# A hybrid trunk layer on one core: the order of its instructions found with another model of the machine

## The chip, the cores and the metric

The kernel runs on one core of a Trainium2 chip. The metric is the device time of one execution in microseconds; the time before is the median of three runs. A profile is one further execution, recorded by the hardware profiler. The engines are TensorE (PE in the profile, its weight loads PEld), VectorE (DVE), ScalarE (ACT), GpSimd (POOL) and SyncE (SP), whose queue issues nearly all the transfers of this kernel.

## The reference

One layer of a streaming encoder over 1024 positions and 1024 channels, in float32:

```python
h = rms_norm(x, norm1_w)
q, k, v, g_ret, x_lru, y_lru, gate_ret, gate_lru = split(h @ w_in)
o = head_group_norm(chunkwise_retention(rotary(q), rotary(k), v), ret_gn_w)
y_a = (o * silu(g_ret)) @ w_ret_o
hl = rg_lru(causal_depthwise_conv(x_lru, ...), ...)
y_b = (hl * gelu(y_lru)) @ w_lru_o
mix = sigmoid(gate_ret + b0) * y_a + sigmoid(gate_lru + b1) * y_b
x = x + mix @ w_out
gate, val = split(rms_norm(x, norm2_w) @ ffn_w_up)
x = x + (gelu(causal_depthwise_conv(gate, ...)) * val) @ ffn_w_down
return rms_norm(x, norm_f_w)
```

Retention has four heads and is done in chunks with a state carried over; the recurrence (`rg_lru`) has block-diagonal gates and a scan over positions. The inner width of the last block is 3072.

## The kernel before

**Precision and products.** Every large product splits both operands in a high part (rounded to the fp32r format) and a low part (the rest): `split` (L164 to L169) does one cast on ScalarE (L167) and one subtraction on VectorE (L168). Three matmuls (high times high, high times low, low times high) then stand for one in float32. Tiles are 128 x 512.

**Jobs.** The work is a list of jobs, each a 256 x 1024 piece of output from a 256-column piece of a weight matrix: 28 jobs of the input projection, four for each of the two branch outputs, 24 up jobs (one 128-wide piece of the gate and one of the value) and 12 down jobs. A standard job (`mm_std`, L316) takes 96 matmuls at L330. Most are fast ones (`mm_fast`, L377): a Strassen-like scheme of seven products instead of eight on 2 x 2 blocks, 84 matmuls at L387, 12 for each product. It needs sums of blocks (L246 to L262 on VectorE for weights; `tsets`, L539 to L556, or `x_sums` for the other operand) and combines products: `keep` (L399 to L403) copies a PSUM bank on ScalarE (L402), `more` adds what is accumulated (L408), `total` (L411 to L414) adds a bank on VectorE (L413). After a copy the same bank goes on accumulating the next-but-one product. There are six banks for jobs and two for the rest (tile `a`). There are 61 fast jobs in all.

**Weights.** `loads` (L199) fetches raw blocks over SyncE's queue (L208), `preps` (L224) splits them; `pump` keeps up to six raw and seven split blocks ahead in 22 buffers `w`. All other tiles live in 81 buffers `u`; the buffer that each takes is chosen by the kernel's Python code while it writes the program.

**Background work.** After a job its `post` may leave a generator in `back`: the recurrence (`lru_block`, matmuls at L814, the product stored at L853), rotary, retention and their output. `advance` writes some of it between the products of later jobs. Operands for the next stage come from `builders`: `operand` loads tiles (L997 from the stored branch output, L1230 from the down weights) and splits them, and writes the sums. `build` and `need` do this, and `keep`, `total` and the weights' `pump` after the first job do their part, inside `hp()`, which raises the priority by an offset of 1500 instructions.

**After the branches.** The merge projection (L1182) adds the input and stores the sum, then comes the second norm with its transposes (L513). In the up stage `post_ff` (L1207 to L1224) does the convolution (L1212, L1215, L1217), GELU (L1218) and the product (L1219) and stores it through GpSimd's queue (L1220). The down stage loads those as "weights" (L208) and accumulates three groups of four jobs over the stored sum; the last group ends with the final norm (L1286 to L1302).

**What sets the order.** The program is written as one list of instructions. When the `TileContext` closes, the toolchain gives each engine and queue its own list: it runs the program through a model of the machine and puts down each instruction when, by that model, the data that it reads is there and the buffer that it writes is free; among several, the one with the higher priority goes first (program order, moved by `hp()`). Waits are then added where one engine depends on another. Within a queue the order is fixed from then on.

## Time and profile before

| | |
|---|---|
| median of three runs | 1673.02 us (1672.82, 1673.02, 1676.43) |
| the profiled execution | 1675.42 us |
| its span, first to last instruction | 1673.6 us |
| mean granted TensorE clock | 0.994 |
| instructions | 21183 |
| moved by transfers | 225.97 MB, 135 GB/s |

The span is what the trace covers; the 1.82 us between it and the execution's own time lie around it. Busy time of an engine is the time in which at least one of its instructions is recorded; for TensorE records overlap, since matmuls are pipelined. In lists of instructions, `x` is the count of merged ones, and the square bracket gives the time that the engine stood idle before the first of them, with what ended it. A line such as `ACT u L402 <- PE g L387` means: ScalarE's instruction of line 402 waited for TensorE's of line 387. `SPq` is an instruction that issues a transfer.

### The profile page before, as it was taken

How to read it: one execution, taken by the hardware profiler on the slowest of the kernel's cores; microseconds unless marked ns; L12 is line 12 of the kernel's file. 1: busy time of each engine (PE TensorE's matmuls, PEld its weight loads, DVE VectorE, ACT ScalarE, POOL GpSimd, SP SyncE). 2: the span in 40 equal slices, each digit the busy share in tenths (PEclk: the TensorE clock that was granted, in tenths of full speed). 3: DMA queues.
4: the chain of work that ended last, by engine and by line, in shares of the span. 5: the costliest groups of instructions: out<-in, count | busy, mean ns of one | idle time of the engine just before them, and what ended most of it. 6: DMA issues, size and time to landing. Idle time of an engine off the chain costs nothing.

```text
span 1673.6 us, 21183 instructions
## 1 busy us (share of the span) xinstructions
PE 1627.2 (97%) x7224; PEld 1332.6 (80%) x7224; DVE 1289.9 (77%) x2366; ACT 886.4 (53%) x1480; POOL 40.7 (2%) x60
## 2 busy tenths in 40 slices
PE   8999999999999999999999999999999999999997
PEld 6888788888888877887778788888888887777776
DVE  8998768666888889857862796777767777878886
ACT  7654444535678877753530564444444455444554
POOL 0001000000000000000000000000000000000000
PEclk9999999999999999999999999999999999999999
DMA  7243212131333348656463022222222237687851
GB/s 293 89 154 97 86 54 89 51 95 45 113 114 105 122 140 267 210 166 232 154 209 107 32 95 82 82 82 82 89 82 82 92 122 229 224 260 243 260 193 76
DMA packets 120524, 225.97 MB, mean 135 GB/s; under 512 B 14048, under 2 KB 14176, under 8 KB 120416
## 3 DMA queue, kind: packets, MB, share of 16 engines
q1 hardware_dynamic: 116192, 210.99, 39.1%
q0 software_dynamic: 4224, 13.64, 2.1%
q8 instruction: 56, 0.92, 0.2%
q14 instruction: 52, 0.43, 0.1%
HBM read 164.80 MB, written 54.53 MB: 131 GB/s over the span
## 4 chain that ended last, share of the span: by engine, by line
PE 50%; DVE 8%; DMA 6%; ACT 3%; issue 2%; SPq 0%; DVEq 0%; ACTq 0%
PE g L387 36%; PE g L330 7%; PE g L1182 4%; DMA u<-w_dn 2%; DVE u L168 2%; PE a L814 2%; DVE w L168 1%; DMA w<-ff_d 1%; DMA x_d<-u 1%; DVE u L797 1%; ACT u L167 1%; DVE u L413 1%; DMA u<-u_d 1%; PE a L513 0%; DMA u<-w_out 0%
## 5 line engine op out<-in xcount | busy, mean ns | idle before, releaser
L387 PE MATMUL g<-u,w 128*128 128x512 f32 x5124 | 1204.7, 393 | 20.1 <-ACT u L402 9.7
L387 PEld LDWEIGHTS g<-u,w 128*128 128x128 f32 x5124 | 958.9, 188 | 224.6 <-ACT u L402 14.8
L167 ACT CAST w<-w 128x512 fp32r<-128x512 f32 x471 | 291.3, 621 | 359.7 <-PE g L387 280.6
L168 DVE TENSOR_TENSOR w<-w,w 128x512 fp32r<-128x512 f32 x471 | 322.6, 686 | 90.0 <-ACT w L167 85.4
L330 PE MATMUL g<-u,w 128*128 128x512 f32 x960 | 227.2, 394 | 2.8 <-ACT u L167 2.8
L167 ACT CAST u<-u 128x512 fp32r<-128x512 f32 x232 | 139.3, 620 | 150.1 <-DVE u L552 16.1
L330 PEld LDWEIGHTS g<-u,w 128*128 128x128 f32 x960 | 181.3, 190 | 41.9 <-ACT u L167 3.2
L168 DVE TENSOR_TENSOR u<-u,u 128x512 fp32r<-128x512 f32 x232 | 154.5, 687 | 38.8 <-ACT u L167 25.9
L413 DVE TENSOR_TENSOR u<-g,u 128x512 f32<-128x512 f32 x183 | 125.6, 686 | 57.0 <-PE g L387 43.5
L402 ACT COPY u<-g 128x512 f32<-128x512 f32 x183 | 106.4, 582 | 73.8 <-PE g L387 73.7
L1182 PE MATMUL g<-u,u 128*128 128x512 f32 x384 | 90.1, 392 | 2.5 <-ACT u L167 1.6
L1182 PEld LDWEIGHTS g<-u,u 128*128 128x128 f32 x384 | 71.3, 188 | 18.4 <-ACT u L167 2.0
L1215 DVE SCALAR_TENSOR_TENSOR u<-u,par,u 128x511 f32<-128x511 f32 (+1 forms) x96 | 71.6, 747 | 6.2 <-ACT u L1212 5.5
L1220 POOL DMA_DIRECT2D ff_d<-u x48 | 36.2, 753 | 1271.0 <-DVE u L1219 1271.0
L246 DVE TENSOR_TENSOR w<-w,w 128x512 f32<-128x512 f32 x61 | 42.1, 690 | 20.6 <-DMA w<-w_up 12.6
L814 PE MATMUL a<-u,u 128*128 128x512 f32 x192 | 48.8, 394 | 4.3 <-ACT u L167 3.5
L1184 DVE TENSOR_TENSOR u<-g,u 128x512 f32<-128x512 f32 x16 | 11.1, 691 | 49.3 <-PE g L1182 49.3
L1212 ACT ACTIVATE u<-u,par 128x512 f32<-128x512 f32 x48 | 39.1, 817 | 15.7 <-DVE u L413 15.7
L814 PEld LDWEIGHTS a<-u,u 128*128 128x128 f32 x192 | 35.5, 188 | 14.3 <-ACT u L167 5.6
L249 DVE TENSOR_TENSOR w<-w,w 128x512 f32<-128x512 f32 x61 | 42.0, 688 | 0.9
L262 DVE TENSOR_TENSOR w<-w,w 128x512 f32<-128x512 f32 x61 | 41.9, 686 | 0.4
L255 DVE TENSOR_TENSOR w<-w,w 128x512 f32<-128x512 f32 x61 | 41.8, 685 | 0.3
(173 smaller groups left out, 1151.2 us busy)
## 6 DMA issues: line engine op xcount, KB each, us to landing
w<-w_in SPq DMA_DIRECT2D x112, 256.0 KB, 2.7
w<-w_up SPq DMA_DIRECT2D x96, 256.0 KB, 2.6
u<-w_dn SPq DMA_DIRECT2D x96, 256.0 KB, 4.0
u<-x_d SPq DMA_DIRECT2D x56, 256.0 KB, 5.3
x_d<-u SPq DMA_DIRECT2D x48, 256.0 KB, 3.3
ff_d<-u POOLq DMA_DIRECT2D x48, 256.0 KB, 2.5
w<-ff_d SPq DMA_DIRECT2D x48, 256.0 KB, 3.8
u<-x SPq DMA_DIRECT2D x32, 256.0 KB, 5.3
```

Source lines behind the costliest of these rows:

```text
L167: S.copy(hi, src)
L168: V.tensor_sub(lo, src, hi.bitcast(F32))
L246: V.tensor_add(s1, a21, a22)
L249: V.tensor_sub(s1, s1, a11)
L262: V.tensor_sub(s1, a12, s1)
L330: PE.matmul(ps[h], w[a][:, c], o[b], start=n == 0, stop=n == 23)
L387: PE.matmul(bank, w[a][:, c], need(op, (bn, j))[b], start=first and n == 0, stop=n == 11, skip_group_check=True)
L402: S.copy(u, bank)
L413: V.tensor_add(u, bank, u)
L814: PE.matmul(ps, wg[g][a][:, cs], xs[k][b], start=q == 0, stop=q == 5)
L1182: PE.matmul(ps, o[a][:, 128 * t:128 * t + 128], wo[k][b], start=n == 0, stop=n == 23)
L1215: V.scalar_tensor_tensor(c[:, s:], src[:, :TH - s], w, c[:, s:], ALU.mult, ALU.add)
```

## The change

The context is opened with one more argument. The kernel's own code is the same, line for line: the same instructions on the same engines with the same operands and buffers. The model that is run to find the order is the toolchain's timeline model in place of its core simulator, which is the default. The two count the time of instructions, transfers and queues in their own ways; the rule by which an instruction is put down is the same.

```diff
--- before.py
+++ after.py
@@ -1372,7 +1372,7 @@
     args = {n: nc.dram_tensor(n, v.shape, mybir.dt.from_np(v.dtype), kind="ExternalInput").ap()
             for n, v in arrays.items()}
     y = nc.dram_tensor("out", (T, D), F32, kind="ExternalOutput").ap()
-    with tile.TileContext(nc) as tc:
+    with tile.TileContext(nc, schedule_with_timeline_sim=True) as tc:
         tile_trunk_layer(tc, **args, out=y)
     r = run_bass_kernel_spmd(nc, [arrays], core_ids=[0])
     return r.results[0]["out"].reshape(1, T, D)
```

## The prediction

> **What bounds the kernel now.** I read the page first, for who is busy.
>
> ```profile
> span 1673.6 us, 21183 instructions
> PE 1627.2 (97%) x7224; PEld 1332.6 (80%) x7224; DVE 1289.9 (77%) x2366; ACT 886.4 (53%) x1480; POOL 40.7 (2%) x60
> PE 1627.2 (97%) x7224; PEld 1332.6 (80%) x7224; DVE 1289.9 (77%) x2366; ACT 886.4 (53%) x1480; POOL 40.7 (2%) x60
> PE 1627.2 (97%) x7224; PEld 1332.6 (80%) x7224; DVE 1289.9 (77%) x2366; ACT 886.4 (53%) x1480; POOL 40.7 (2%) x60
> PE 1627.2 (97%) x7224; PEld 1332.6 (80%) x7224; DVE 1289.9 (77%) x2366; ACT 886.4 (53%) x1480; POOL 40.7 (2%) x60
> ```
>
> TensorE has work in 1627.2 of 1673.6 us, so the idle time is 46.4 us, and that is the first ceiling on what any order can win: no instruction is added, removed or resized. The profiled execution took 1675.42 us, 1.82 us more than its span, and lies 2.40 us above the median of the three runs, 1673.02. What I sum below is a difference against 1675.42 and is carried over to the median.
>
> A busy TensorE is not yet a full one, since a matmul's record is longer than the step from one to the next. So I took the step from the chain of waits, in its longest unbroken piece:
>
> ```profile
> 976.34 413.68 PE g L387 x1825
> ```
>
> 413.68 / 1825 = 0.2267 us for one matmul of 512 columns. Then I cut the span by stage: input projections (to 638), the recurrence's end and the two output projections (638 to 860), the merge projection with the second norm (860 to 976), up (976 to 1390), and down. The columns are the stretch, its length, then busy time and count of TensorE, its weight loads, VectorE, ScalarE and GpSimd, then granted clock, DMA share and GB/s.
>
> ```profile
> core 0: us, PE busy (x) PEld busy (x) DVE busy (x) ACT busy (x) POOL busy (x), PEclk, DMA share, GB/s
> 0.00:30.00 30.00, 23.95 (x94) 19.32 (x95) 23.15 (x37) 23.64 (x42) 0.20 (x4) 1.00 0.97 355
> 30.00:500.00 470.00, 468.05 (x2168) 386.01 (x2168) 375.71 (x797) 253.21 (x430) 4.30 (x8) 1.00 0.29 91
> 500.00:638.00 138.00, 135.61 (x594) 110.67 (x593) 121.83 (x204) 108.25 (x158) 0.00 (x0) 1.00 0.41 132
> 638.00:660.00 22.00, 18.79 (x79) 14.22 (x77) 19.17 (x36) 14.48 (x26) 0.00 (x0) 1.00 0.86 291
> 660.00:760.00 100.00, 99.93 (x441) 82.75 (x442) 72.61 (x120) 64.79 (x87) 0.00 (x0) 1.00 0.60 193
> 760.00:860.00 100.00, 92.44 (x385) 73.09 (x384) 87.25 (x143) 47.33 (x82) 0.00 (x0) 0.97 0.62 206
> 860.00:976.00 116.00, 115.44 (x536) 93.67 (x535) 63.10 (x126) 35.97 (x66) 0.00 (x0) 1.00 0.23 76
> 976.00:1390.00 414.00, 414.00 (x1828) 342.83 (x1827) 301.82 (x495) 204.70 (x344) 33.90 (x45) 1.00 0.29 95
> 1390.00:1445.00 55.00, 47.28 (x189) 37.82 (x188) 44.42 (x75) 25.33 (x44) 2.27 (x3) 0.91 0.71 233
> 1445.00:1515.00 70.00, 66.74 (x292) 54.28 (x291) 57.67 (x94) 33.91 (x60) 0.00 (x0) 1.00 0.73 235
> 1515.00:1645.00 130.00, 125.14 (x548) 102.24 (x548) 108.31 (x200) 63.61 (x122) 0.00 (x0) 1.00 0.65 211
> 1645.00:1673.60 28.60, 19.81 (x87) 15.74 (x85) 14.90 (x47) 11.22 (x26) 0.00 (x0) 0.94 0.29 110
> ```
>
> Count times 0.2267, taken from the length, gives the slack of a stage whose matmuls are all 512 wide. 0 to 30: 94 are 21.3, slack 8.7. 500 to 638: 594 are 134.7, slack 3.3. 638 to 660: 79 are 17.9, slack 4.1. 660 to 760: 441 are 100.0, none. 760 to 860: 385 are 87.3, slack 12.7. 976 to 1390: 1828 are 414.4, none. 1390 to 1445: 189 are 42.8, slack 12.2. 1445 to 1515: 292 are 66.2, slack 3.8. 1515 to 1645: 548 are 124.2, slack 5.8. The last 28.6 us: 87 are 19.7, slack 8.9. The stretches 30 to 500 and 860 to 976 hold narrower matmuls, so there I take idle time, 470.00 - 468.05 = 1.95 and 116.00 - 115.44 = 0.56. Together 62.0 us. The first 8.7 are input loads and the first splits, the last 8.9 the final norm and the stores, and a different order shortens neither by much. In between lie 44.4 us, of which 24.9 sit in two stretches, 760 to 860 and 1390 to 1445. So: TensorE bounds the kernel; an order can win at best some 44 us (2.7%) and can lose without such a limit.
>
> [...]
>
> **What the change does.** It adds and removes no instruction, transfer or byte. The toolchain places each instruction on its engine or queue when a model of the machine says that its inputs are there and its buffer is free, the most urgent first; the change swaps that model. Buffer numbers, the urgent blocks and the moment at which a load is asked for are fixed earlier by the kernel's own code, so they stay. On the chip each engine then runs its list strictly in that order. So the cost is made of places where the list and the chip disagree: an engine stands at an instruction whose input isn't there while ready work lies behind it. The trace is full of such places:
>
> ```profile
> L167 ACT CAST w<-w 128x512 fp32r<-128x512 f32 x471 | 291.3, 621 | 359.7 <-PE g L387 280.6
> L168 DVE TENSOR_TENSOR w<-w,w 128x512 fp32r<-128x512 f32 x471 | 322.6, 686 | 90.0 <-ACT w L167 85.4
> L402 ACT COPY u<-g 128x512 f32<-128x512 f32 x183 | 106.4, 582 | 73.8 <-PE g L387 73.7
> ```
>
> ```profile
> ACT w L167 <- PE g L387: 280.6, 204, 4.3
> ```
>
> 204 of 471 weight splits on ScalarE stood waiting for TensorE to release the buffer, 280.6 us in all. That is harmless as long as weights are ahead of TensorE, as they are from 976 to 1390, where slack is nil. I cost every edit there at nothing: its cover is the seven split blocks kept ahead, the matmuls of one block taking 12 x 0.2267 = 2.72 us, and if the cover were gone TensorE would wait for a cast of 0.621 us and a subtraction of 0.686 us per block.
>
> Outside of it three long gaps of TensorE matter, and each shows what an order decides.
>
> First gap, the last store of the recurrent branch, in the timeline around it:
>
> ```profile
> 753.47 0.68 DVE L852 TENSOR_TENSOR u<-u,u 128x512 f32<-128x512 f32 x1
> 754.03 5.92 SPq L997 DMA_DIRECT2D u<-u_d  x11
> 761.05 0.32 SPq L853 DMA_DIRECT2D u_d<-u  x1
> 769.68 1.52 PE L330 MATMUL g<-u,w 128*128 128x512 f32 x2 [2.78 <-ACT u L167]
> ```
>
> ```profile
> 770.00:775.00 5.00, 5.00 (x12) 3.67 (x12) 2.56 (x5) 1.94 (x4) 0.00 (x0) 0.50 0.67 199
> ```
>
> The product that the store writes is done at 753.47 + 0.68 = 754.15, but SyncE issues eleven loads ahead of the store, which goes out at 761.05, 6.9 us late. TensorE's last operand comes through that store, a reload and a split, and TensorE stands 2.78 us. Then its clock is at 0.50 for 5 us: 12 matmuls where 5.00 / 0.2267 = 22 would fit, 10 x 0.2267 = 2.3 us lost. The gap is worth 2.78 + 2.3 = 5.1 us. If the store moves before the loads, all of it goes, and what is late next are the eleven loads, each by the 0.32 us that the store's issue takes; they feed operands that are used after the one that TensorE lacked. If the store stays behind the loads (both are ready, and the loads are marked urgent), nothing is won; if it slips behind another such batch, it costs up to another 5.92 us. I take the 5.1, the end nearer to the row that shows the product ready and the queue free to choose.
>
> [...]
>
> Second and third gap, at the start of down, TensorE's groups and ScalarE's instructions:
>
> ```profile
> 1399.57 1.52 PE L330 MATMUL g<-u,w 128*128 128x512 f32 x6
> 1405.09 8.35 PE L387 MATMUL g<-u,w 128*128 128x512 f32 x24 [4.01 <-ACT u L402]
> 1413.29 20.56 PE L330 MATMUL g<-u,w 128*128 128x512 f32 x90
> 1440.50 50.96 PE L387 MATMUL g<-u,w 128*128 128x512 f32 x215 [3.71 <-ACT u L1218]
> ```
>
> ```profile
> 1402.73 0.62 ACT L167 CAST u<-u 128x512 fp32r<-128x512 f32 x1 [2.54 <-DVE u L1217]
> 1403.26 0.63 ACT L1218 ACTIVATE u<-u 128x512 f32<-128x512 f32 x1
> 1403.94 0.62 ACT L167 CAST u<-u 128x512 fp32r<-128x512 f32 x1
> 1404.46 0.58 ACT L402 COPY u<-g 128x512 f32<-128x512 f32 x1
> ```
>
> At 1399.57 + 1.52 = 1401.09 TensorE has finished the product whose bank must be copied (L402). The copy runs only at 1404.46, because ScalarE stood 2.54 us at a split that waited for VectorE and had three operations queued ahead of the copy. TensorE waits 4.01 us, and its next 24 matmuls take 1413.29 - 1405.09 = 8.20 us instead of 5.44, another 2.76. With the copy at 1401.1 the gap would be the copy's own 0.58: 3.4 us and, without the long gap, 2.76 of clock come back, 6.2 us. The two bounds are 0, if the split stays ahead, and 6.8, if the bank's user moves too; below nothing if another two splits go ahead of the copy, 2 x 0.62 = 1.2 us. This is the wait on a wrong guess of when VectorE is done, so it is the kind that another model changes; I take 6.2. The third gap (3.71 us before 1440.50) ends a stretch in which VectorE is busy 44.42 of 55.00 us; the work is there in any order, so I take 0, with 3.7 as the other end.
>
> What is given back: a new order makes small misses of its own. The two rows
>
> ```profile
> PE g L387 <- ACT u L402: 9.7, 7, 4.0
> PE a L814 <- ACT u L167: 3.5, 4, 1.6
> ```
>
> are of the kind, 11 waits of 13.2 us in all, 9.2 without the 4.0 that is the second gap. I take 3.3 us, the slack of 500 to 638, a stretch whose small misses come from the recurrence's matmuls (L814); the bounds are 0 and 9.2.
>
> Sum: -5.1 - 6.2 + 3.3 = -8.0 us. 1675.4 - 8.0 = 1667.4 for the profiled execution, 1673.0 - 8.0 = 1665.0 for the median.
>
> **The rivals.** *Slower, through late copies.* A Strassen-like job of 84 matmuls copies a bank three times (183 copies, 582 ns each), and each copy has the next 12 matmuls, 2.72 us, as cover. 2.72 - 0.58 = 2.1 us is the margin, used up when four of ScalarE's casts (0.62 us each) lie ahead of the copy. From that point TensorE stands, at every job. If one copy in eight comes 1 us late, 23 x 1 = 23 us: 1696; if one in four, 46 us: 1719. For it: it happens already, seven times, 9.7 us, and a model in which casts come ready earlier, or ScalarE has room earlier, puts more of them ahead of a copy. Against: ScalarE is busy only 204.70 of 414.00 us in the up stage. Price taken: 23 us.
>
> *No change.* The three gaps end in chains whose work is given (VectorE 44.42 of 55.00 us, a store and reload through memory), urgency decides between ready instructions as before, and small misses cancel: 1673, within 3.3 us of it. Here too belongs that the change does not do what it says, if both models give the same order; with 21183 instructions timed differently that is unlikely, a chance of 0.03 in the 0.18 below.
>
> *A large gain.* All three gaps go and half of the rest between the ends: 5.1 + 6.8 + 3.7 + (44.4 - 15.6) / 2 = 30 us, 1643. Against it: VectorE's share in the same stretches.
>
> **How the numbers follow.** About 0.2%, 3.3 us, is what a measurement of this kernel can tell from no change. The forecast gets 0.40, the large gain 0.04: faster 0.44. No change 0.18. Slower 0.38, most of it from late copies, spread from 1677 to above 1719. The forecast's own range takes both gaps at their larger ends with nothing given back and the third gap too (5.1 + 6.8 + 3.7 = 15.6, and some 5 of the other slack): 1652; its upper end is the bound of no change, 1669.7. Below 1652 lies about 0.06. Upwards I cover the late copies to 29 us, a little past one in eight, leaving about 0.12 out: 1702. The likeliest is only a little ahead of its opposite; the time named is its own.
>
> **What would show it.** Right: busy counts unchanged, no gap over 2 us between 760 and 800 with the last L853 store ahead of most L997 loads, and the copy near 1401 following its product within 1 us. The step on the third gap is wrong if VectorE's busy time there shrinks because its work moved into the up stage. The step on the up stage is wrong if 414 us of it hold clearly fewer than 1828 matmuls. The forecast falls if waits of TensorE for L402 grow beyond 9.7 us by more than the gaps give, or if weights (w) arrive late anywhere; then the sign is the other one.

## The result, and the profile after

The changed kernel takes 1723.03 us (median of four runs, 1722.23 to 1726.03), the kernel before 1674.72 on the same chip (1672.82 to 1681.41): a ratio of 1.029, with a 95% interval from 1.027 to 1.032. It is slower by 48 us, where 8 us faster were forecast, and lies above the range. The profiled execution took 1722.85 us.

The page of the kernel after, the lines that answer to those of before:

```profile
span 1721.1 us, 21162 instructions
PE 1643.5 (95%) x7224; PEld 1343.0 (78%) x7224; DVE 1276.4 (74%) x2366; ACT 889.5 (52%) x1485; POOL 40.6 (2%) x60
...
L387 PE MATMUL g<-u,w 128*128 128x512 f32 x5124 | 1203.6, 394 | 24.2 <-ACT u L402 14.6
...
L167 ACT CAST w<-w 128x512 fp32r<-128x512 f32 x471 | 286.6, 619 | 351.1 <-PE g L387 194.0
L168 DVE TENSOR_TENSOR w<-w,w 128x512 fp32r<-128x512 f32 x471 | 319.5, 685 | 135.0 <-ACT w L167 130.0
...
L402 ACT COPY u<-g 128x512 f32<-128x512 f32 x183 | 106.1, 581 | 79.9 <-PE g L387 65.3
```

The work is the same: 7224 matmuls, 2366 operations of VectorE, durations within 2 ns of before. ScalarE has five instructions more, all of them table loads, of which more below. TensorE's idle time is 1721.1 - 1643.5 = 77.6 us instead of 46.4. That is 31 us more, and the span grew by 47.5, so a third of the loss, 16.3 us, doesn't show as idle: there TensorE counts as busy while its matmuls don't follow each other at their step. Of these 16.3 us, 9.8 fall where the granted clock is 0.50: there the matmuls lose 17.2 us against their step after and 7.4 before. The mean granted clock fell from 0.994 to 0.984.

So I measure the loss as **slack**: from the start of each TensorE instruction to the next, less the steady step of its kind in the trace of before (0.2267 us for 512 columns, as in the prediction; the median of 0.216 for 256 and 0.108 for 128), summed over a stretch. A wait counts in the stretch in which it ends. The stretches end at work that both kernels have: the first L919 (retention's first product), the last L960 (retention's end), the last L814 (the recurrence's end), the first and the last L1182 (merge projection), the first L1219 (second norm and the first up job) and the first L1270 (start of down). Each column gives the time at which its stretch ends and the slack in it, in us:

| | to first L919 | retention | recurrence | to first L1182 | merge | norm 2 | up | down | sum |
|---|---|---|---|---|---|---|---|---|---|
| end, before | 159.4 | 427.2 | 731.8 | 846.9 | 940.2 | 976.9 | 1439.7 | 1673.6 | |
| slack, before | 3.8 | 6.1 | 8.3 | 9.7 | 4.8 | 1.3 | 7.1 | 16.7 | 57.7 |
| end, after | 168.7 | 480.4 | 782.5 | 899.0 | 990.4 | 1038.5 | 1476.6 | 1721.1 | |
| slack, after | 7.3 | 31.5 | 29.0 | 4.6 | 11.3 | 11.8 | 2.7 | 6.0 | 104.3 |
| difference | +3.5 | +25.4 | +20.7 | -5.1 | +6.5 | +10.5 | -4.4 | -10.7 | +46.6 |

The sum of the differences, 46.6, is the 47.5 us of the span but for 0.9. By this table the change won 20.2 us (up to the merge, up, down) and lost 66.6, most of it in retention and recurrence. These two are the background work, which is written between the main products.

What went wrong in retention is seen in one step of it. A step makes scores (L919, TensorE), masks them (L921, VectorE) and multiplies with the values (L924, TensorE). In the timeline of before:

```profile
234.50 0.38 PE L919 MATMUL a<-u,u 128*128 128x128 f32 x2
234.64 0.95 PE L387 MATMUL g<-u,w 128*128 128x512 f32 x3
234.92 0.29 DVE L921 TENSOR_TENSOR sm<-a,cst 128x128 f32<-128x128 f32 x1 [1.98 <-PE a L919]
235.32 0.58 ACT L402 COPY u<-g 128x512 f32<-128x512 f32 x1
235.42 0.61 PE L924 MATMUL a<-u,sm 128*128 128x256 f32 x2
```

From L919 to L924 go 235.42 - 234.50 = 0.92 us, and three main matmuls fill them. In the timeline of after:

```profile
266.46 0.38 PE L919 MATMUL a<-u,u 128*128 128x128 f32 x2
266.60 3.70 PE L387 MATMUL g<-u,w 128*128 128x512 f32 x15
266.98 0.28 DVE L921 TENSOR_TENSOR sm<-a,cst 128x128 f32<-128x128 f32 x1
270.13 0.59 PE L924 MATMUL a<-u,sm 128*128 128x256 f32 x2
...
274.75 0.70 PE L924 MATMUL a<-u,sm 128*128 128x256 f32 x2 [0.49 <-DVE sm L921]
...
276.86 0.58 ACT L402 COPY u<-g 128x512 f32<-128x512 f32 x1 [0.58 <-PE a L919]
...
277.32 0.70 PE L924 MATMUL a<-u,sm 128*128 128x256 f32 x2 [0.49 <-DVE sm L921]
...
278.53 3.10 PE L387 MATMUL g<-u,w 128*128 128x512 f32 x12
```

The mask is done at 267.26, but in TensorE's list 15 main matmuls stand ahead of L924, so the step takes 270.13 - 266.46 = 3.67 us. Behind it TensorE's list holds no main matmul until 278.53, and the steps of retention follow each other bare, one every 277.32 - 274.75 = 2.57 us, with TensorE standing 0.49 us at each L924. Meanwhile a main product has ended whose bank needs its copy (L402); the copy waits for an L919, by the names one that still reads the buffer that it writes, and runs only at 276.86. On the chip the main matmuls at 278.53 don't wait for it, they stand there by the list; whether the model put them there because of that copy isn't shown. First too much stands between the steps, then nothing. Over all 32 such steps the lists hold a median of 3 TensorE instructions between L919 and its L924 before (3 to 8), and 12 after: 12 to 21 in 17 of them, 0 in the other 15.

In the recurrence it is ScalarE. The timeline of after, ScalarE's lines and TensorE's wait behind them:

```profile
716.28 1.28 ACT L817 ACT_TABLE_LOAD   x1
717.58 0.69 ACT L817 ACTIVATE u<-a,par 128x512 f32<-128x512 f32 x1
718.29 1.28 ACT L837 ACT_TABLE_LOAD   x1
719.58 0.63 ACT L837 ACTIVATE u<-u 128x512 f32<-128x512 f32 x1
720.23 1.28 ACT L825 ACT_TABLE_LOAD   x1
721.53 0.72 ACT L825 ACTIVATE u<-u,lt 128x512 f32<-128x512 f32 x1
...
735.42 1.28 ACT L817 ACT_TABLE_LOAD   x1
736.72 0.69 ACT L817 ACTIVATE u<-a,par 128x512 f32<-128x512 f32 x1
737.44 0.72 ACT L825 ACTIVATE u<-u,lt 128x512 f32<-128x512 f32 x1
737.46 1.58 PE L814 MATMUL a<-u,u 128*128 128x512 f32 x5 [3.71 <-ACT u L817]
```

Sigmoid (L817), Tanh (L825), Exp (L831) and Sqrt (L837) of neighbouring steps alternate, and ahead of 44 of their 80 instructions ScalarE loads a table, 1.28 us each time, about twice the 0.63 to 0.72 us of the activation itself; the L825 at 737.44, behind an L817, has no load. Beside the load itself little is spent: the one at 718.29 starts 0.02 us after the activation before it (717.58 + 0.69 = 718.27) and the next activation 0.01 us after the load. There are 81 of them after and 76 before. Five more, 6.4 us, are not 20.7; whether it is the place at which they stand that costs, the experiments have to say.

### The profile page after: what moved, and what is told of

It reads as the page before. It is cut to its first block, busy times and chain, and to the rows that moved or that the text cites. A ratio compares the mean times of both kernels' runs of the same rounds, so it can differ in the third digit from the quotient of the medians.

```text
span 1721.1 us, 21162 instructions
## 1 busy us (share of the span) xinstructions
PE 1643.5 (95%) x7224; PEld 1343.0 (78%) x7224; DVE 1276.4 (74%) x2366; ACT 889.5 (52%) x1485; POOL 40.6 (2%) x60
## 4 chain that ended last, share of the span: by engine, by line
PE 38%; issue 12%; DVE 5%; DMA 3%; ACT 2%; POOL 1%; SPq 0%; POOLq 0%; DVEq 0%; ACTq 0%
PE g L387 25%; PE g L330 7%; PE g L1182 5%; DVE u L168 1%; POOL ff_d L1220 1%; DMA u<-w_dn 1%; PE a L814 1%; DMA u<-w_out 1%; DVE w L168 0%; ACT u L167 0%; DMA t_d<-u 0%; DVE u L797 0%; DMA u<-x_d 0%; ACT L817 0%; DMA u<-og_d 0%
## 5 line engine op out<-in xcount | busy, mean ns | idle before, releaser
L387 PE MATMUL g<-u,w 128*128 128x512 f32 x5124 | 1203.6, 394 | 24.2 <-ACT u L402 14.6
L167 ACT CAST w<-w 128x512 fp32r<-128x512 f32 x471 | 286.6, 619 | 351.1 <-PE g L387 194.0
L402 ACT COPY u<-g 128x512 f32<-128x512 f32 x183 | 106.1, 581 | 79.9 <-PE g L387 65.3
L1182 PE MATMUL g<-u,u 128*128 128x512 f32 x384 | 90.4, 396 | 9.2 <-ACT u L167 9.2
L1182 PEld LDWEIGHTS g<-u,u 128*128 128x128 f32 x384 | 72.9, 191 | 24.8 <-ACT u L167 9.6
L814 PE MATMUL a<-u,u 128*128 128x512 f32 x192 | 49.8, 400 | 6.3 <-ACT u L817 3.7
L246 DVE TENSOR_TENSOR w<-w,w 128x512 f32<-128x512 f32 x61 | 42.0, 688 | 14.3 <-DMA w<-w_in 6.9
L814 PEld LDWEIGHTS a<-u,u 128*128 128x128 f32 x192 | 36.7, 192 | 15.0 <-ACT u L817 4.1
L1212 ACT ACTIVATE u<-u,par 128x512 f32<-128x512 f32 x48 | 39.1, 816 | 9.5 <-DVE u L413 9.5
L1218 ACT ACTIVATE u<-u 128x512 f32<-128x512 f32 x48 | 30.4, 634 | 24.8 <-DVE u L1215 14.9
L249 DVE TENSOR_TENSOR w<-w,w 128x512 f32<-128x512 f32 x61 | 41.9, 687 | 0.6
L255 DVE TENSOR_TENSOR w<-w,w 128x512 f32<-128x512 f32 x61 | 41.9, 686 | 0.5
```

The costliest lines, as they stand in the source:

```text
L167: S.copy(hi, src)
L246: V.tensor_add(s1, a21, a22)
L249: V.tensor_sub(s1, s1, a11)
L387: PE.matmul(bank, w[a][:, c], need(op, (bn, j))[b], start=first and n == 0, stop=n == 11, skip_group_check=True)
L402: S.copy(u, bank)
L814: PE.matmul(ps, wg[g][a][:, cs], xs[k][b], start=q == 0, stop=q == 5)
```

## The experiments

Two ways of editing are used. One holds an engine's list: after the program is written, each instruction of that engine is tied to the one before it in a stored order, by a dependency that makes no wait. In the cuts the stored orders are written as names.

```diff
+def _pin(nc, tc, eng, code):
...
+            tc.add_manual_dep(tr[at], prev.name,
+                              mybir.DependencyInfo(mybir.DependencyClass.NoSync, mybir.DependencyReason.DATA),
+                              reason="pin")
```

The other changes the timeline model while the order is found, and puts it back at once.

**Whose list is it?** Three kernels hold lists of one kernel in the other. The first:

```diff
     with tile.TileContext(nc, schedule_with_timeline_sim=True) as tc:
         tile_trunk_layer(tc, **args, out=y)
+        _pin(nc, tc, mybir.EngineType.PE, ORDER_OF_BEFORE)
```

> The changed kernel (all lists worked out with the timeline model), but TensorE's list is held to the one of before, instruction by instruction; the lists of the other engines are worked out around it. Theory A (the time is lost in TensorE's own list: a step of the background, L924 behind L919, is put down behind 12 to 21 main matmuls where before it stood behind 3 to 8): the loss of 48 us goes, 1655 to 1685 us, last L960 before 440 us. Theory B (the loss is in the lists of ScalarE and VectorE, which put the copies L402 and the evictions down too late): these lists stay those of the timeline model, so 1705 to 1730 us and last L960 after 465 us. Theory C (SyncE's list, late loads) says the same as B.

It took 1745.07 us (ratio to before 1.043, 1.041 to 1.045). Retention's slack fell to 18.2 and its end to 454.7, between the marks of the two theories, but the recurrence's slack rose to 38.5, and TensorE now waited for copies, as its waits show (total in us, times, longest):

```profile
PE g L387 <- ACT u L402: 38.3, 15, 6.1
```

The same with the sides exchanged, TensorE's list of after in the kernel before:

```diff
     with tile.TileContext(nc) as tc:
         tile_trunk_layer(tc, **args, out=y)
+        _pin(nc, tc, mybir.EngineType.PE, ORDER_OF_AFTER)
```

> The kernel before (lists worked out with the core simulator), but TensorE's list is held to the one of after; the other engines' lists are worked out around it by the core simulator. Theory A (TensorE's list): it loses most of what the change lost, 1700 to 1735 us, last L960 after 465 us. Theories B and C (lists of ScalarE and VectorE, or of SyncE): within 10 us of before, 1665 to 1685 us, last L960 before 440 us.

1776.93 us (1.061, 1.060 to 1.063), worse than any theory had it. And with ScalarE's and VectorE's lists held to those of before, under the timeline model:

```diff
     with tile.TileContext(nc, schedule_with_timeline_sim=True) as tc:
         tile_trunk_layer(tc, **args, out=y)
+        _pin(nc, tc, mybir.EngineType.Activation, ORDER_OF_BEFORE)
+        _pin(nc, tc, mybir.EngineType.DVE, ORDER_OF_BEFORE)
```

> The changed kernel, but ScalarE's and VectorE's lists are held to those of before; TensorE's and SyncE's are worked out by the timeline model around them, and the median number of TensorE instructions between L919 and its L924 stays 11 (after 12, before 3). Theory A (TensorE's list): still slow, 1700 to 1740 us. Theory B (lists of ScalarE and VectorE): 1660 to 1685 us.

1802.37 us (1.076, 1.074 to 1.079). A was right only that this one stays slow; as the one cause it falls with the first run. B and C fall with the second, which they had within 10 us of before, and B with the third too. All three times lie above every range. Every mixture is worse than either whole, so a list found in one company lost in another, and these runs can't price an engine's list by itself. My reading is that a copy stands where its own model run had the product ending, and that the loss has to be looked for in the model that makes all the lists; why the mixtures lose as much as they do was not taken further.

**The down stage alone.** All lists of before, but what the program has from the conv step of the twentieth of the 24 up jobs on stands, on each engine, in the order of after among itself.

```diff
     with tile.TileContext(nc) as tc:
         tile_trunk_layer(tc, **args, out=y)
+        for engine, order in BEFORE_THEN_AFTER.items():
+            _pin(nc, tc, engine, order)
```

> The kernel before with every engine's list held to the one of before, except that the instructions written from the second half of the up stage's conv steps on (the last of the up stage and the down stage) stand among themselves in the order of after. If what the change gained in the down stage (4 us of slack there instead of 22) is a matter of the lists of that stage alone: 18 us less than before, 1652 to 1662 us, and no gap at 1405 and 1500 us. If it came only from the later start of that stage, which gave its loads more time: 1668 to 1680 us.

1662.27 us (0.993, 0.991 to 0.995), 11 us faster than before. Up and down together have 5.7 us of slack (-0.1 and 5.8), before 23.8: 18 us less, as the first of the two theories had it, and the span is 14.9 us shorter. The time lies 0.3 us above that theory's range and 6 below the other's. Its timeline at the place of the second and third gap, TensorE's groups and the copy:

```profile
1402.26 2.88 PE L387 MATMUL g<-u,w 128*128 128x512 f32 x12
...
1404.98 5.15 PE L330 MATMUL g<-u,w 128*128 128x512 f32 x22
1405.34 0.57 ACT L402 COPY u<-g 128x512 f32<-128x512 f32 x1
1409.96 5.60 PE L387 MATMUL g<-u,w 128*128 128x512 f32 x24
```

The product of 12 ends at 1402.26 + 2.88 = 1405.14, its copy starts at 1405.34, and the next matmuls follow with no gap: 22 standard matmuls of the other kind cover the copy.

**The model's queues.** The timeline model has a setting for how many instructions an engine may hold that have been issued and can't run yet, and by my reading of it the list of an engine is the order of issue. The core simulator, by the same reading, has no such queue: an instruction is put down when it can run. My estimate was that this makes the distances of 12 to 21. These places are settings of the model; how many instructions an engine of the chip holds, no run here measured. The next three runs make the modelled queues short:

```diff
+    from concourse import hw_specs
+    depth = hw_specs.TRN2Spec.ENG_ISSUE_QUEUE_DEPTH
+    was = dict(depth)
+    depth.update({mybir.EngineType.PE: 1})
     with tile.TileContext(nc, schedule_with_timeline_sim=True) as tc:
         tile_trunk_layer(tc, **args, out=y)
+    depth.update(was)
```

The other two set 1 for `Activation` and `DVE`, and for all three.

> The changed kernel, but while the order is worked out the timeline model may hold 1 issued instruction of TensorE in its queue instead of 35 (ScalarE and VectorE keep 12). The instructions of TensorE between L919 and its L924 fall from a median of 12 to 4, each head's retention from 147 to 250 list places to 128. Theory A1 (the depth of TensorE's modelled queue alone carries the loss): 1655 to 1685 us. Theory A2 (every modelled queue carries a part; the run with TensorE's list held to before's lists stayed at 1745 us with the queues of ScalarE and VectorE at 12): 1700 to 1750 us. Theory B (the model's durations, not its queues): 1715 to 1750 us, and the next two runs too.

> The changed kernel with the modelled queues of ScalarE and VectorE at 1 instead of 12, TensorE's kept at 35. TensorE's list keeps distances of 13 to 24 at L919 to L924. Theory A1: 1710 to 1750 us. Theory A2: less than the change but still slow, 1690 to 1720 us. Theory B: 1715 to 1750 us.

> The changed kernel with the modelled queues of TensorE, ScalarE and VectorE all at 1: an instruction is put down only when its engine can start it. All else of the timeline model stays. Theories A1 and A2 (the queues carry the loss): 1655 to 1685 us, retention's last L960 before 440 us. Theory B (durations, and what else the timeline model prices in another way): 1715 to 1750 us.

One place for TensorE: 1912.37 us (1.139), for ScalarE and VectorE: 1724.54 (1.028, 1.025 to 1.031), for all three: 1924.24 (1.146). The middle one says that the queues of ScalarE and VectorE carry nothing that shows beside TensorE's full queue, so A2 falls. The other two no theory had: the highest range ended 160 us too low for the first and 174 for the third. The distance from L919 to L924 did fall to a median of 4, so something else had come in: in the first, TensorE waited 33 times for a copy (L402), 160.0 us in all, against 9.7 before. The longest of these waits, with ScalarE's lines and two of VectorE's:

```profile
83.29 0.68 DVE L249 TENSOR_TENSOR w<-w,w 128x512 f32<-128x512 f32 x1
84.06 0.62 ACT L167 CAST w<-w 128x512 fp32r<-128x512 f32 x1 [13.46 <-DVE w L249]
84.70 1.28 ACT L735 ACT_TABLE_LOAD   x1
...
93.77 0.42 DVE L734 TENSOR_SCALAR u<-u 128x512 f32<-128x512 f32 x1
94.22 0.63 ACT L735 ACTIVATE u<-u 128x512 f32<-128x512 f32 x1 [8.24 <-DVE u L734]
94.76 0.60 ACT L167 CAST w<-w 128x512 fp32r<-128x512 f32 x1
95.27 0.58 ACT L402 COPY u<-g 128x512 f32<-128x512 f32 x1
95.90 1.65 PE L387 MATMUL g<-u,w 128*128 128x512 f32 x3 [17.88 <-ACT u L402]
```

VectorE's list has one part of the rotary tables (L694 to L734) ahead of a sum of weights (L249) and the next part behind it; ScalarE's has a cast that waits for that sum and an activation (L735) that waits for the tables, both ahead of a copy, and TensorE stands 17.88 us. My reading is that these lists fit a slower TensorE, since with one place the model can't take a matmul while another runs, and that one place so tests another thing than the queue's depth. No run shows the model from inside, so this stays argued.

**A short queue, and priced loads.** The second thing in which the two models differ, again by my reading, which no run shows from inside: the core simulator charges a table load where an activation needs it, the timeline model never does. The next runs take 4 places, then a model that charges loads, then both, and the last measures what the loads cost in the list of after as it stands.

```diff
-    depth.update({mybir.EngineType.PE: 1})
+    depth.update({mybir.EngineType.PE: 4})
```

> The changed kernel, with 4 places in the timeline model's queue for TensorE instead of 35 (the others keep 12). The run with one place went far to the other side (1912 us), so theory D is now: what loses is a deep modelled queue, a list that is filled far ahead of the moment at which an instruction can run, and one place is a case of its own, because the model's TensorE then can't take a matmul while the one before it runs and all other lists are laid out for a slower TensorE. D: with 4 places the median distance of L919 to L924 is 5 (before 3, after 12): 1665 to 1690 us, last L960 before 440 us. Theory E (the model doesn't price the table loads of ScalarE, ACT_TABLE_LOAD 1.28 us each, 81 of them in the changed kernel): still above 1705 us. If neither holds, above 1705 us here and in the next two runs.

```diff
+    was, now = timeline_sim._needs_act_table_load, [()]
...
+    def needs_load(func):
+        f = str(func).split(".")[-1]
+        if f in ("Identity", "Copy", "Square") or f in now[0]:
+            return False
+        now[0] = next(s for s in sets if f in s)
+        return True
+
+    timeline_sim._needs_act_table_load = needs_load
     with tile.TileContext(nc, schedule_with_timeline_sim=True) as tc:
```

In this edit `Identity`, `Copy` and `Square` are charged no load. The traces agree: none of the 76 loads of before and the 81 of after stands at a line with one of these three functions (L492, L793, L1212 and L1286 among them, or the copies of L402).

> The changed kernel, with the full queues (35 and 12), but the timeline model charges a table load wherever an activation needs another table than the one before it; nothing is changed on the chip but the order. Theory E alone: 1665 to 1690 us. Theory D alone: 1710 to 1730 us. Both carry a part: 1695 to 1712 us.

Both edits together, with 8 for the 4:

> The changed kernel with both: 8 places for TensorE in the modelled queue, and table loads charged. Theories D and E, each for a part, and the down stage's gain of the change kept: 1640 to 1668 us, faster than before. D alone or E alone: like the better one of the two runs ahead, within 6 us. If the timeline model's order is worse for another reason than these: above 1690 us.

And the lists of after, all held, with other functions, so that the kernel computes another thing; one of the eight lines:

```diff
-                S.activation(th[m], th[m], AF.Sqrt)
+                S.activation(th[m], th[m], AF.Sigmoid)
```

> The changed kernel with every engine's list held to the one of after, but the functions of L735, L736, L772, L825, L831, L837, L1075 and L1218 (Sin, Gelu, Tanh, Exp, Sqrt, Silu) are all Sigmoid, so that the lists hold 17 table loads instead of 81; what the kernel computes is another thing. This is the price of the loads in the lists as they stand. Theory E: 20 to 35 us less than after, 1688 to 1703 us. Theory D alone, the loads lie in idle time of ScalarE: 1713 to 1725 us.

The medians: 1687.13 us with 4 places (1.008, 1.005 to 1.011), 1713.38 with priced loads (1.022, 1.019 to 1.025), 1667.00 with 8 places and priced loads (0.995, 0.994 to 0.996), 1697.10 with few loads in the lists of after (1.013, 1.010 to 1.015). The first, third and fourth lie in the ranges of D, of both, and of E. The second lies in the range of D alone, 1.4 us above that of both, so by itself it doesn't bear out E; what a model that charges loads is worth beside the full queue is some 10 us. The slack by stretch says where each counts:

| slack, us | to first L919 | retention | recurrence | to first L1182 | merge | norm 2 | up | down | sum |
|---|---|---|---|---|---|---|---|---|---|
| after | 7.3 | 31.5 | 29.0 | 4.6 | 11.3 | 11.8 | 2.7 | 6.0 | 104.3 |
| 20 places | 8.5 | 20.3 | 33.9 | 3.3 | 8.0 | 6.6 | 3.5 | 5.8 | 90.1 |
| 4 places | 6.9 | 2.9 | 19.0 | 13.0 | 2.1 | 0.3 | 8.4 | 15.7 | 68.4 |
| loads priced | 6.0 | 29.3 | 17.0 | 8.9 | 11.1 | 11.8 | 3.1 | 8.8 | 96.0 |
| 8 places, loads priced | 6.5 | 3.7 | 6.9 | 6.9 | 8.1 | 0.3 | 6.7 | 12.1 | 51.3 |
| after, few loads | 5.4 | 31.8 | 6.1 | 1.0 | 10.8 | 11.8 | 2.8 | 9.0 | 78.7 |
| before, few loads | 4.5 | 6.2 | 6.7 | 12.3 | 6.0 | 1.2 | 6.1 | 15.0 | 58.0 |

Retention and the second norm answer to the queue alone: 31.5 to 2.9 and 11.8 to 0.3 with 4 places, and next to nothing from the loads. In the norm the longest wait, 3.4 us, is for VectorE's work (L518) on the transposes (L513), which may be again a short step between long ones; that wasn't taken further. The recurrence answers to both. The row of retention and that of the recurrence in the cut of TensorE by stretch, of the kernel after:

```profile
168.70:480.40 311.70, 294.42 (x1355) 0.99 0.21 63
480.40:782.50 302.10, 284.29 (x1208) 0.97 0.46 149
```

With 4 places:

```profile
162.60:435.60 273.00, 273.00 (x1311) 1.00 0.24 69
435.60:742.60 307.00, 293.67 (x1273) 0.99 0.46 149
```

And in the lists of after with few loads:

```profile
166.90:478.90 312.00, 294.79 (x1354) 0.99 0.22 63
478.90:758.00 279.10, 275.17 (x1207) 0.99 0.50 162
```

With 4 places retention is 38.7 us shorter; 44 of its matmuls, 10.0 us, now stand elsewhere, and the rest is slack. With few loads the recurrence is 23.0 us shorter with one matmul less, and retention is as long as it was.

**Controls, and the best of both.** Three more runs: one takes the loads out of the lists of before, by the same eight lines; one holds the lists of the run with 8 places and priced loads, with the order of after from the twentieth up job's conv step on; and one sets 20 places for the 4.

> The control to the run with few table loads: the kernel before, every engine's list held to its own, and the same eight lines' functions replaced by Sigmoid, so that what it computes is another thing; 22 table loads instead of 76. Theory E (the core simulator prices the loads, so its lists leave room for them): at most 5 us less than before, 1666 to 1675 us, and the recurrence's stretch gains under 3 us. If loads cost the same in any list: 20 to 35 us less, 1640 to 1655 us.

> The lists of the run with 8 places and priced loads (1667 us), but the last conv steps of the up stage and the down stage stand among themselves in the order of after. On the up and down stage that run lost 19 us of TensorE time, the run that took this stage from after lost 6. If what a stage loses hangs on its own lists: 13 us less, 1650 to 1658 us, the fastest. If it hangs on the state in which the stage before leaves the buffers: 1663 to 1670 us.

> The changed kernel with 20 places in the timeline model's queue for TensorE (4 places gave 1687 us, 35 give 1723 us); the median distance of L919 to L924 is 13, with places of 0 among them as in after. Theory D, by the size of the queue: between the two, 1695 to 1718 us. If only the full queue loses: within 6 us of 1687 us.

The control took 1673.79 us, before 1676.18 on that chip (0.999, 0.997 to 1.000): 54 loads fewer gain 2.4 us there, while in the lists of after 64 fewer gain 1723.0 - 1697.1 = 26. So it is the place of a load that costs, not their number: TensorE's slack is 57.7 us with the loads of before and 58.0 without. The lists made with priced loads say the same: they hold 91 loads, ten more than after, and lose 17.0 us in the recurrence instead of 29.0. The best kernel took 1658.26 us (0.991, 0.989 to 0.992), 0.3 us above the range of the first of its two theories: 1 and 7.9 us of slack in up and down. Of the 13 us that this theory expected, some 9 came. 20 places took 1707.28 us (1.019, 1.018 to 1.021), between 1687 and 1723, so from 4 places on the loss grows with the queue. By stretch that holds for retention and the norm; the recurrence loses more with 20 places (33.9) than with the full queue (29.0). 8 places without priced loads weren't run, so how much of the last 20 us of the best model comes from 8 places instead of 4 is open.

## Why the prediction was wrong

- **The ceiling.** That an order can win some 44 us at best and can lose without such a limit: no run here goes against either. The best won 18 us, the worst lost 245.
- **The up stage costs nothing.** It held. The 7.1 us of the table's up stretch before are the second gap, which lies in it (6.9 us from 1401 to 1414); up to 1390 there is none. The 2.7 after stand in its first 21 us, right behind the norm.
- **First gap, -5.1.** The gap went, by the mechanism forecast. The product that the last store writes and the store itself, in the timelines of VectorE and of SyncE's queue after:

```profile
798.64 0.68 DVE L852 TENSOR_TENSOR u<-u,u 128x512 f32<-128x512 f32 x1
```

```profile
799.35 0.32 SPq L853 DMA_DIRECT2D u_d<-u  x1
800.18 0.49 SPq L997 DMA_DIRECT2D u<-u_d  x1
```

  The store goes out 0.03 us after its product, ahead of 14 of the 32 loads that L997 makes of `u_d`, where before it stood ahead of 4. The stretch lost 4.6 us instead of 9.7; that the difference is 5.1 again is in part chance, since its other waits changed too (two of 1.5 us after, of 0.9 and 1.2 before). What got late behind it, and the prediction didn't see, is the merge projection, which begins with a wait of 9.2 us for split weights, before 1.6. The table counts it in the merge (+6.5), so the two stretches together lose 15.9 us instead of 14.5: the won gap came back at the next place.
- **Second gap, -6.2.** The mechanism held, and the size nearly: by slack the gap was 6.9 us, and nothing is left of it. One reading was wrong. The prediction took the six standard matmuls that end at 1401.09 for the product to be copied, but L402 copies products of fast jobs alone, and the last of these ended at 1384.63 + 15.10 = 1399.73:

```profile
1384.63 15.10 PE L387 MATMUL g<-u,w 128*128 128x512 f32 x65
```

  So a copy in time has the six matmuls as cover, and the 0.58 us that the prediction left don't remain. After:

```profile
1464.86 2.88 PE L387 MATMUL g<-u,w 128*128 128x512 f32 x12
1467.58 5.15 PE L330 MATMUL g<-u,w 128*128 128x512 f32 x22
1467.78 0.59 ACT L402 COPY u<-g 128x512 f32<-128x512 f32 x1 [1.38 <-PE g L387]
```

  The copy starts 0.04 us after its product's end, 1467.74, and ScalarE stood ready for it.
- **Third gap, 0.** This was wrong, to the kernel's gain: it cost 5.6 us of slack before (1439.7 to 1446) and is gone after. VectorE's load there was no reason for it to stay. Up and down together won 23.8 - 8.7 = 15.1 us, and the run with the order of after for this stage alone won 11 us of device time.
- **What is given back, +3.3.** This is the step that failed. It was taken from a small-miss stretch of before, with 9.2 as the upper bound; it was 66.6 us. The rows of before can't bound it, since they show the misses of other lists. The step rested on the sentence that each instruction is put down when by the model its data is there, and on the one ahead of the prediction that this rule is the same in both models. It is not, by my reading: the timeline model puts an instruction down when the queue takes it, which may be ahead of the moment at which it can run, and it charges no table load. The runs show what each is worth, though not the model from inside. Of the 48.3 us of device time, a short queue takes back 35.9 (1723.0 - 1687.1), and few table loads take back 25.9; the two together, in the run with 8 places and priced loads, 56.0, which is more than the loss, as the won stages partly stay. These times come from different chips; by the ratios to before on each, the three are 36.0, 27.8 and 57.6. The first two add to more than the third; both count in the recurrence, where either alone takes back 10 us or more.
- **The rival with the other sign.** Late copies were priced at 23 us, and at 46 for one copy in four, which is nearly the result. But the copies are not where it went: TensorE's waits for L402 are 14.6 us after, 9.7 before. The margin that the rival counted, four casts ahead of a copy, was not the one that broke here, and at the late copy shown above TensorE didn't wait. With one modelled place it was the copies, 160.0 us.
- **What the diff could have told.** A change of model is a change of every assumption in it, and the prediction weighed only where the two would disagree on durations. That a program of 21183 instructions would be timed differently it said; how, it left open, and then summed as if small.

## What to carry to other kernels

A scheduler's list is good only if the model behind it holds what the chip does: ask which costs it leaves out (here the table loads, 26 us) and how far it issues ahead of what can run (here 36 us), before asking how exact its durations are. Background work with short hops between engines shows it first; count the instructions between a producer and its consumer in the list, and compare them with the time that the hop takes (here 0.92 us, with three main matmuls in it). Where one order is better in one stage and another in the next, take each for its own stage, all engines together: that made 1662 us of 1673 and 1723, and 1658 of 1667 and 1723, while the lists of one or two engines in the others' company lost in all three runs.

## What the runs showed of the hardware

Behind which gap TensorE's clock falls, the length of the gap alone doesn't tell here. In the kernel after, behind a gap of 1.45 us, with waits of 1.03 and 0.31 us in the 4 us ahead of it, and behind one of 2.32 us, the cut of the 2 us that follow (granted clock behind the count):

```profile
548.29:550.29 2.00, 2.00 (x5) 0.50 0.00 0
667.82:669.82 2.00, 2.00 (x9) 1.00 0.59 187
```

And in the kernel before, behind one of 2.30 us:

```profile
1595.73:1597.73 2.00, 2.00 (x9) 1.00 0.68 262
```

Five matmuls behind the shortest of the three gaps, nine behind the other two. What else decides it wasn't shown. In the records of the granted clock of before and after, but for the end of the span, it stays at 0.50 for 3.41 us (six times), 6.83 (five times) or 10.24 (once) at a time, which are one, two and three times the same length. Three gaps of 3.1 to 4.5 us in these two traces are followed by eight main matmuls or more: the first eight took 0.447 us a step behind the 4.01 us before 1405.09 and 0.353 behind the 3.71 before 1440.50 (before), and 0.448 behind the 3.44 before 1023.32 (after), against 0.227.
